# Hybrid attention trunk on one core: loads at the stages' turns, a copy on ScalarE, sums of squares on VectorE, stores in pairs, wider warming products

## The chip, the core and the metric

The kernel runs on one core of a Trainium2 chip. Times are device microseconds (us) of one execution. The engines are named as in the profile: PE is TensorE's matmul, PEld its weight load, DVE is VectorE, ACT is ScalarE, POOL is GpSimd, SP is SyncE, which issues most DMAs. L12 is line 12 of the kernel.

## What is computed

One layer over x (1024 x 2048, float32), with a second input p (1024 x 256):

```python
hn = rmsnorm(h, norm_mix_g); proj = hn @ w_in        # q, k, v, gate of 8 + 8 heads
sb_out = stick_breaking_attention(sb_q, sb_k, sb_v)   # sigmoids and a running product
df_out = differential_attention(rope(df_q), rope(df_k), df_v, lam)  # softmax1 - lam * softmax2
df_out = rmsnorm(df_out, subln_g) * (1 - lambda_init)
mixed = concatenate([sb_out * silu(sb_g), df_out * silu(df_g)])
h = h + mixed @ w_out
gate = sigmoid(rmsnorm(h, norm_ple_g) @ w_ple_gate)
out = rmsnorm(h + gate * (p @ w_ple_proj), norm_final_g)
```

## The kernel before

**Products.** Activations lie transposed, 128 features x 512 tokens to a tile; the 1024 tokens are two halves. Each float32 operand is split into two fp32r parts: ScalarE casts the high part, VectorE subtracts it from the original for the low part. Each product is then three matmuls: high x high, high x low, low x high (in the q/k projection L251 to L253). Most of the 11110 matmuls are these. The projections to v and gate, to the output, and to the last gate take Strassen's form with seven block products, A11, A12, S2, S1, S3, S4, A22 (class `Seven`): sums of blocks come from VectorE, and a result that is finished later is added up in DRAM or out of `part_d`.

**Stages, in time.** (1) v and gate for all 16 heads, up to about 640 us, both phases `ph` of 16 units; the four u's of a product are summed into PSUM tiles `pbc`, `pc`. (2) The heads of half 1, which attend to 512 keys, then, from about 1070 us ("the middle"), those of half 0, which attend to 1024, half 1's keys and values among them (kept in DRAM). For each head PE runs the q/k projection of that head as a stream of 32 groups of three matmuls (`unit`), and between the groups the attention of the head before it. `ORDER` alternates a differential head (`df`) and a stick-breaking head (`sb`); one such pair takes about 72 us in half 0. (3) From about 1650 us the output projection (8 units), (4) from about 2010 us the gate projection with products p1/p2 (A11, A12), p6 (S2), p5 (S1), p3 (S4), the S3 product, and A22, (5) final norm and stores.

**What sets the order.** PE's order is written out by hand (`manual_schedule`). Inside a head, `Side` holds steps with due times: after each group of three matmuls `side.tick()` runs what is due, and the table TICK (L41 to L54) gives the times in ticks. So a number in TICK decides behind which other instruction of its own engine a cast, a copy or a subtraction is issued; each engine takes its instructions in that order. In the Seven stages a slot (`op.slot`, `gv.slot`) is one block product; `soon` holds functions for a later slot, `xq` the operands to be loaded and split. SP issues its DMAs in order, each when its tile is free.

**The places that the change and the prediction touch:**
- Start: `warm` (L857) makes 24 products of the ones matrix, 128 columns each, while the first operands are loaded; the first real product is L647 to L649 (`Seven.product`), and L628 casts the first operands.
- Chores (L1043): from slot 36 of stage 1 on, w_out and parts of w_in are split ahead of time: slots of remainder 0 by three load a tile, of remainder 1 cast it and subtract (`chi`, `clo`, L1055), of remainder 2 store both to DRAM. L1110 adds PSUM's `pbc` to `s` in the last units of that stage.
- `wprep` (L160) loads a piece of w_in into `wraw`, casts `whi` (L172) and makes or loads `wlo` (L168, L174); `Stream` hands these out.
- Attention (a helper, L300 on): `scores` make z; for an sb head `weights` issues the sigmoids L358/L359, the scan L365 and the product L369; for a df head the masked minimum L382, the exponential L390 (`et`), the factors L395/L396 and the scaling L397, L402. `values` transposes v (L417), copies its high part (L419), subtracts its low part (L422). `turn` transposes weights (`tp`, L437), `parts` splits them (`lead`, `awh`: L455/L456; `awl`: L460/L461); `mix` multiplies them with v (`av`, L479 to L484) and sums the result (L495, L498; `avb`); `squared` (L511 to L514) makes `sqv`, `sqh`.
- A head's q and k (`taken`): for a df head they are copied from `acc` by ScalarE, rotated on VectorE (L1451 to L1454), cast (L1431, L1433, L1435) and their low parts subtracted (L1440). For an sb head q is copied by ScalarE (L1399), k is multiplied with `rstd` on VectorE (L1403: `qk<-acc,ssa`). v and gate of a head are loaded and multiplied with `rstd` (L1385).
- Output projection: `wf` tiles (`wfhi`, `wflo`, loads L1323) come from `wout_d`; the last head's result `mixed_d` is stored in L280; L647 to L649 read the weights.
- Gate stage: `norm` (L1770) multiplies two tiles of partial sums of squares with the ones matrix into one PSUM tile (L1775), and `load_sums` (L1790) loads the two tiles. `p6` (L1898) loads `part_d[u]` into `s` (L1902), forms S2's product, and adds (L1905); L1913 adds the product of p5. `gprod` is L1762 to L1764. `first_load` (L1518) loads both k halves of a weight block, `gate_operand` (L1234) the operands. 
- End: the last quarter of the output is transposed, scaled by the row's root (`leave`, L2169: L2174 on ScalarE, L2176 on VectorE), and stored by 8 DMAs (L2179, L2182); `finals` (L1986/L1987) adds and stores the columns ahead of it.

## Time and profile before

| | us |
|---|---|
| three timed runs | 2359.87, 2366.0, 2360.83 |
| their median | 2360.83 |
| the profiled execution, its own time | 2364.5 |
| its span | 2362.7 |
| busy: PE, DVE, ACT, POOL | 2324.6, 1796.3, 1269.2, 296.0 |
| granted TensorE clock, mean | 0.995 |
| DMA, mean | 236 GB/s |

A row of the list of waits reads: engine, tile and line that waited, what released it, then total us, how many times, the longest. A row of the table by stretch reads: start and end, length, then the busy time of PE, PEld, DVE, ACT, POOL with the count of instructions in brackets, then the granted clock of TensorE (1.00 is full), the DMA engines' busy share and GB/s. A row in order of time reads: start, busy time, engine, line, operation, output and inputs, shapes, and in square brackets the idle time before it and who ended that. A row of DMA issues ends with KB each and the us from issue to landing.

### The profile page before, as it was taken

The numbers are of one execution on the slowest core, as the hardware profiler recorded it, in microseconds if no ns is written. First come the engines' busy times: TensorE is split into PE (matmuls) and PEld (weight loads), VectorE is DVE, ScalarE is ACT, GpSimd is POOL, SyncE is SP. The second block draws the span as 40 slices with busy tenths as digits, with TensorE's granted clock in tenths as the row PEclk, the third lists the DMA queues.
The fourth block names the chain that finished last, engine by engine and source line by source line (L and its number), as shares of the span: only waits on it lengthen the run. The fifth ranks groups of instructions, "written<-read, shape, count | busy, mean of one in ns | idle before, by whom it ended". The sixth has DMA issues, their size and how long they took to land. (4 is left out here: it accounts for less than half of the span.)

```text
span 2362.7 us, 32655 instructions
## 1 busy us (share of the span) xinstructions
PE 2324.6 (98%) x11110; PEld 1937.1 (82%) x11110; DVE 1796.3 (76%) x3115; ACT 1269.2 (54%) x2305; POOL 296.0 (13%) x439
## 2 busy tenths in 40 slices
PE   9999999999999999999999999999899999999998
PEld 7878878888788888887888888888778887788787
DVE  7487786656578888877877877778687887687787
ACT  6323253333357776777767676677533434533455
POOL 2121111111100000000011100111021121111000
PEclk9999999999999999999999999999999999999999
DMA  8586798766787777787567666668798788998965
GB/s 263 205 292 230 256 302 219 196 144 131 208 276 245 248 249 256 256 302 241 197 194 212 180 188 209 196 196 255 220 248 213 245 242 267 307 353 271 327 201 183
DMA packets 255544, 556.66 MB, mean 236 GB/s; under 512 B 28544, under 2 KB 40064, under 8 KB 255376
## 3 DMA queue, kind: packets, MB, share of 16 engines
q1 hardware_dynamic: 186112, 396.18, 50.7%
q0 software_dynamic: 52848, 128.74, 22.3%
q10 hardware_dynamic: 16416, 29.65, 3.5%
q8 instruction: 87, 1.43, 0.2%
q14 instruction: 81, 0.66, 0.1%
HBM read 359.16 MB, written 203.69 MB: 238 GB/s over the span
## 5 line engine op out<-in xcount | busy, mean ns | idle before, releaser
L740 ACT CAST wpr<-T 128x512 fp32r<-128x512 f32 x208 | 127.2, 621 | 484.5 <-DVE T L699 402.2
L251 PE MATMUL acc<-xh,whi 128*128 128x512 f32 x768 | 314.5, 410 | 3.4 <-DVE qk L1403 3.2
L253 PE MATMUL acc<-xh,wlo 128*128 128x512 f32 x768 | 302.2, 393 | 0.9 <-DVE wlo L168 0.5
L252 PE MATMUL acc<-xl,whi 128*128 128x512 f32 x768 | 301.2, 392 | 0.0
L253 PEld LDWEIGHTS acc<-xh,wlo 128*128 128x128 f32 x768 | 144.6, 188 | 34.5 <-DMA wlo<-wlo_d 1.2
L251 PEld LDWEIGHTS acc<-xh,whi 128*128 128x128 f32 x768 | 145.2, 189 | 28.0 <-DVE qk L1403 3.6
L252 PEld LDWEIGHTS acc<-xl,whi 128*128 128x128 f32 x768 | 145.4, 189 | 23.5 <-issue 0.2
L172 ACT CAST whi<-wraw 128x1024 fp32r<-128x1024 f32 x128 | 134.6, 1052 | 23.8 <-DMA wraw<-w_in 9.3
L754 DVE TENSOR_TENSOR wpr<-T,wpr 128x512 fp32r<-128x512 f32 x208 | 142.5, 685 | 5.9 <-ACT wpr L740 2.7
L853 POOL DMA_DIRECT2D vg_d<-hc x128 | 89.1, 696 | 456.4 <-DVE hc L1072 267.3
L740 ACT CAST wpr<-wraw 128x512 fp32r<-128x512 f32 x128 | 78.8, 617 | 114.8 <-DMA wraw<-tw_d 35.6
L390 ACT ACTIVATE et<-z,mx 128x512 f32<-128x512 f32 (+7 forms) x128 | 94.7, 740 | 62.8 <-DVE mx L382 62.7
L456 ACT CAST awh<-tp 128x256 fp32r<-128x256 f32 (+1 forms) x160 | 81.0, 507 | 78.7 <-PE tp L437 78.7
L382 DVE CUSTOM_DVE_ANT_0 z<-z,wide 128x512 f32<-128x512 f32 (+7 forms) x128 | 97.5, 762 | 17.9 <-PE z L335 16.3
L461 DVE TENSOR_TENSOR awl<-tp,awh 128x256 fp32r<-128x256 f32 (+1 forms) x160 | 92.2, 576 | 23.6 <-ACT awh L456 21.2
L365 DVE TENSOR_TENSOR_SCAN pt<-pt 128x511 f32<-128x511 f32 (+3 forms) x64 | 86.7, 1355 | 28.2 <-ACT pt L358 27.6
L754 DVE TENSOR_TENSOR wpr<-wraw,wpr 128x512 fp32r<-128x512 f32 x128 | 86.9, 685 | 26.3 <-ACT wpr L740 26.2
L168 DVE TENSOR_TENSOR wlo<-wraw,whi 128x1024 fp32r<-128x1024 f32 x56 | 68.3, 1220 | 12.8 <-ACT whi L172 12.4
L358 ACT ACTIVATE pt<-z,rcol 128x511 f32<-128x511 f32 (+3 forms) x64 | 47.5, 742 | 52.7 <-DVE z L345 52.2
L484 PE MATMUL av<-awl,v 128*128 128x256 f32 x256 | 72.9, 285 | 1.5 <-DVE awl L461 1.5
L482 PE MATMUL av<-awh,v 128*128 128x256 f32 x256 | 72.4, 283 | 0.1
L483 PE MATMUL av<-awh,v 128*128 128x256 f32 x256 | 72.5, 283 | 0.0
(571 smaller groups left out, 6925.3 us busy)
## 6 DMA issues: line engine op xcount, KB each, us to landing
wraw<-w_in SPq DMA_DIRECT2D x128, 512.0 KB, 4.6
wlo<-wlo_d SPq DMA_DIRECT2D x72, 512.0 KB, 3.4
wraw<-w_vg SPq DMA_DIRECT2D x143, 256.0 KB, 3.6
vg_d<-hc POOLq DMA_DIRECT2D x128, 256.0 KB, 4.9
wlo_d<-wlo SPq DMA_DIRECT2D x56, 512.0 KB, 3.2
wraw<-w_gate SPq DMA_DIRECT2D x92, 256.0 KB, 5.5
h_d<-hc POOLq DMA_DIRECT2D x56, 256.0 KB, 4.9
wraw<-w_out SPq DMA_DIRECT2D x56, 256.0 KB, 4.5
```

Source lines behind the costliest of these rows:

```text
L172: side.later(1, lambda: A.copy(hi[:, o], raw[:, o]))
L251: T.matmul(acc[c], hi[:, k2, kh, c, :], xh, start=first, stop=False)
L252: T.matmul(acc[c], hi[:, k2, kh, c, :], xl, start=False, stop=False)
L253: T.matmul(acc[c], lo[:, k2, kh, c, :], xh, start=False, stop=last)
L365: V.tensor_tensor_scan(pt[:, w], pt[:, w], pt[:, w], initial=1.0, op0=ALU.mult, op1=ALU.bypass)
L382: V.tensor_tensor_reduce(z[:, vw], z[:, vw], add, -DF_SCALE, 3.0e38, ALU.add, ALU.min, mx)
L390: A.activation(et[:, vw], z[:, vw], AF.Exp, bias=mx[:, 0:1], scale=-1.0, accum_out=l[:, c:c + 1])
L456: A.copy(wh[:, o, :], tp[:, o, :])
L461: V.tensor_tensor(wl[:, o, :], tp[:, o, :], wh[:, o, :].bitcast(F32), op=ALU.subtract)
L740: A.copy(t[:, 0], src)
L754: V.tensor_tensor(t[:, 1], src, t[:, 0].bitcast(F32), op=ALU.subtract)
L853: G.dma_start(vg_d[hf, blk, u], o, **(dict(accum_op=ALU.add) if ph else {}))
```

## The change

It has these parts, told in the order of time.
- Warming: 9 products of 512 columns (the ones matrix repeated four times) in place of 24 of 128.
- Chores: a tile is loaded in a slot of remainder 0, cast and subtracted in that of remainder 2, stored in the next of remainder 0; no load in slots 78 to 86.
- The stream's first pieces of w_in are loaded at slots where weight blocks of stage 1 become free (`free`, `Stream.ahead`), rather than with a split `prep`.
- Ticks: the v copies (`vparts`) go from (1, 2) to (3, 4); the df exponential and scaling (`df_soft`) from (1.5, 2, 4.5, 6) to (1, 1.5, 4, 5.5); v and gate of an sb head (`sb_vg`) 2 to 2.5 ticks earlier; q of a df head (`q_turn`) about 2 ticks earlier; two entries of A11 and one of S1 move; the last entry of `begun` goes from 92.5 to 93.5. New entries with "mid_" and "end_" hold the same numbers as those without.
- Middle: in the last pair of the second half of the tokens, an sb head's k is copied by ScalarE and then multiplied on VectorE.
- Gate: the weight block of `first_load` is loaded one k half at a time; the operands of S3 are issued after the latest load in `op.lastw`, and p6's load of `part_d` sets `op.lastw`.
- Norms: one product with the ones matrix; the two sums of squares are added on VectorE two slots after their load is issued (L1822 of the changed kernel).
- End: the stores go out as two of 128 x 1024 and four of 128 x 512 (two column blocks each), and both last `finals` come ahead of them.

```diff
+    "sumlag": 2, "gvx": ((22, 27), (80, 85)), "chore": (36, 78, 87), "opx": (8, 12), ...
-    "parts": (1, 2), "vparts": (1, 2), ... "df_soft": (1.5, 2.0, 4.5, 6.0),
+    "parts": (1, 2), "vparts": (3, 4), ... "df_soft": (1, 1.5, 4, 5.5),
-    "sb_vg": (6, 17, 18, 26, 27.5), "q_turn": (1.5, 5, 7, 8.5, 12, 14, 15.5),
+    "sb_vg": (4, 15, 16, 24, 25.5), "q_turn": (-1.0, 5, 5, 6.5, 10, 12, 13.5),
...
+    def wraw_of(wsrc, pc):
+        raw = wp.tile([P, 2, 2, 2, P], F32, name="wraw", tag="wraw", bufs=2)
+        nc.sync.dma_start(raw, wsrc[pc])
+        return raw
...
+        def ahead(self):
+            self.raws.append(wraw_of(*self.todo[len(self.raws)][:2]))
...
-        for _ in range(24):
-            T.matmul(warm[:, :P], onesr, onesr, start=True, stop=True)
+        for _ in range(9):
+            T.matmul(warm.rearrange("p (a b) -> p a b", a=4), onesr, onesr.unsqueeze(1).to_broadcast([P, 4, P]), start=True, stop=True)
...
+        gv.free = {12: stream.ahead, 21: stream.ahead}
...
         def chore(slot):
-            if slot < CHORE or slot % 3 == 2 and not work:
-                return
-            if slot % 3 == 0 and chores:
+            if slot % 3 == 0 and done:
+                (hi, lo), hi_d, lo_d = done.pop()
...
+            if slot % 3 == 0 and chores and slot >= TICK["chore"][0] and not TICK["chore"][1] <= slot < TICK["chore"][2]:
...
-            elif slot % 3 == 1 and work:
+            elif slot % 3 == 2 and work:
...
-        piece0 = stream.prep(later=True)
         rest_of(prev, True)
-        piece0()
+        stream.prep()
         rest_of(prev, False)
...
-            eng.dma_start(lo.bitcast(F32), src)
+            if nm == "S3":
+                with tc.issue_after(op.lastw.ins):
+                    eng.dma_start(lo.bitcast(F32), src)
+            else:
+                eng.dma_start(lo.bitcast(F32), src)
...
-                            V.tensor_tensor(f, acc[c], rstd, op=ALU.mult)
+                            if seam == "mid_":
+                                A.copy(f, acc[c])
+                                V.tensor_tensor(f, f, rstd, op=ALU.mult)
+                            else:
+                                V.tensor_tensor(f, acc[c], rstd, op=ALU.mult)
...
-            for i, t in enumerate(tiles):
-                T.matmul(ps, ones, t, start=i == 0, stop=i == len(tiles) - 1)
+            T.matmul(ps, ones, out, start=True, stop=True)
...
+            op.soon.append((op.slot + TICK["sumlag"], lambda: V.tensor_tensor(r[0], r[0], r[1], op=ALU.add)))
...
-            nc.sync.dma_start(w, part_d[u])
+            op.lastw = nc.sync.dma_start(w, part_d[u])
...
-        leave(zA[:, 0, :], 0, 0, A)
-        leave(ps[0], 1, 0, V)
-        leave(zA[:, 1, :], 0, 1, A)
-        finals(7)
-        leave(zB[:, 0, :], 2, 0, A)
+        for j in range(2):
+            o = wp.tile([P, 2, HALF], F32, name="ow", tag="wraw", bufs=2)
+            leave(zA[:, j, :], o[:, 0, :], j, A)
+            leave(ps[j], o[:, 1, :], j, V)
+            nc.sync.dma_start(out_of(0, 4, j), o)
...
-        leave(ps[1], 1, 1, A)
-        leave(pt_[0], 3, 0, V)
-        leave(zB[:, 1, :], 2, 1, A)
-        leave(pt_[1], 3, 1, A)
+        for k, t in ((2, [zB[:, j, :] for j in range(2)]), (3, pt_)):
+            for j in range(2):
+                o = ftile()
+                leave(t[j], o, j, (A, V)[j])
+                nc.sync.dma_start(out_of(2 * k, 2, j), o.rearrange("t (c f) -> t c f", c=2))
```

## The prediction

> **What bounds the kernel now.** I read the profile's page first, then the list of TensorE's waits, then the table of busy time by stretch at the places that list names, and last the order in time around each of them.

> ```profile
> span 2362.7 us, 32655 instructions
> PE 2324.6 (98%) x11110; PEld 1937.1 (82%) x11110; DVE 1796.3 (76%) x3115; ACT 1269.2 (54%) x2305; POOL 296.0 (13%) x439
> ...
> PE av L479 <- DVE awl L461: 3.4, 8, 1.6
> PE pa L649 <- DMA wflo<-wout_d: 3.2, 1, 3.2
> PE acc L251 <- DVE qk L1403: 3.2, 1, 3.2
> PE pc L1762 <- DVE hc L1913: 2.7, 1, 2.7
> PE tp L437 <- DVE avb L498: 2.1, 8, 0.3
> ...
> PE av L484 <- DVE awl L461: 1.5, 2, 1.3
> PE pbc L647 <- DVE u L1110: 1.0, 1, 1.0
> ```

> TensorE (PE) is idle for 2362.7 - 2324.6 = 38.1 us of the span; no other engine comes near it. So an edit can win only by issuing less on PE, by shortening one of these waits (columns: total us, times, longest), or by keeping PE's clock up. That last part is in the table by stretch (PE busy in the third column, granted clock after the engines):

> ```profile
> 1069.10:1076.00 6.90, 5.77 (x17) 4.90 (x18) 6.38 (x16) 5.07 (x10) 0.68 (x1) 0.51 0.93 287
> ...
> 1659.70:1663.10 3.40, 3.40 (x15) 3.10 (x15) 1.18 (x3) 0.00 (x0) 0.00 (x0) 0.50 1.06 365
> ...
> 1693.80:1697.20 3.40, 3.40 (x11) 2.72 (x9) 2.18 (x4) 1.86 (x4) 0.85 (x1) 0.50 0.02 3
> ...
> 2222.90:2226.30 3.40, 3.15 (x8) 2.53 (x9) 2.72 (x5) 1.59 (x3) 0.70 (x2) 0.50 1.04 386
> ```

> Behind each of the long waits the clock is halved for 3.4 us, at 1069 for 6.9, twice that; 3.4 us at half clock do 1.7 us less work. So a long wait costs its idle time and 1.7 us more.

> **The change part by part.** The order in which the changed kernel's instructions stand was set beside the old one, engine by engine: PE's order is the same except for the warming products and three norm products that are gone.

> (a) *Start.* 24 warming products of 128 columns become 9 of 512.

> ```profile
> L858 PE MATMUL warm<-onesr x24: 415/415/475, 1.0 to 6.0; 128*128 128x128 f32 x24
> ...
> 6.17 0.73 PE L647 MATMUL pa<-cA11h,wfh 128*128 128x512 f32 x1
> ...
> 10.97 0.43 PE L649 MATMUL pa<-cA11h,wfl 128*128 128x512 f32 x1
> 11.48 0.39 PE L648 MATMUL pa<-cA11l,wfh 128*128 128x512 f32 x1
> 11.70 0.39 PE L649 MATMUL pa<-cA11h,wfl 128*128 128x512 f32 x1
> ...
> 6.15 0.72 ACT L628 ACTIVATE cA11h<-x,gvec 128x512 fp32r<-128x512 f32 x1 [1.34 <-DMA x<-xT]
> ```

> From 6.17 to 10.97 there are eleven steps of about 0.43 us, so nine warmers end near 1.0 + 9 x 0.43 = 4.8, 1.3 us sooner. But the second operand waits for its DMA and exists only at 6.15 + 0.72 = 6.87. If the twelve products still run at half clock behind it, 0.2 us is won; if half of them run at 0.22 us (the step from 11.48 to 11.70), 0.2 + 6 x 0.2 = 1.4. I take 0.5, nearer the first, since PE would stand idle until 6.87 for most of a 3.4 us stretch. [...]

> (b) *Chores at the turn of the first projection.* Loads are left out in slots 78 to 86, and each split comes one slot later.

> ```profile
> 334.15 0.68 DVE L1055 TENSOR_TENSOR clo<-craw,chi 128x512 fp32r<-128x512 f32 x1
> 334.75 0.68 DVE L1110 TENSOR_TENSOR u<-pbc,s 128x512 f32<-128x512 f32 x1
> ```

> PE waits 1.0 us for L1110, behind L1055, which is gone from there: 1.0 us won (0, if another write takes its place, to 1.2).

> (c) *Early w_in loads.* Around 600 to 645 us the order of SP, ScalarE and VectorE is the same, instruction for instruction. 0.

> (d) *Middle: k copied by ScalarE.*

> ```profile
> 1068.43 0.19 ACT L390 ACTIVATION_READ_ACCUMULATOR et<-z,mx 128x1 f32 x1
> 1069.49 0.68 DVE L1403 TENSOR_TENSOR qk<-acc,ssa 128x512 f32<-128x512 f32 x1
> ...
> L1399 ACT COPY qk<-acc 128x512 f32<-128x512 f32 x16 | 9.3, 582 | 0.5 <-PE acc L253 0.5
> ```

> PE is released by L1403's end at 1070.17. The copy stands right behind L390: 1068.52 + 0.58 = 1069.10, so PE goes on 1.1 us sooner. It then works through all of the next 3.4 us, and the second half-clock stretch should fall away: 1.7. Against it, L397 now stands between the copy and L455/L456 and waits for VectorE's L396 behind the rescaled k; awl comes about 1.2 us later, just when PE asks for it, up to 0.7 at half clock. I take 1.1 + 1.7 - 0.6 = 2.2 (0.7, if the second stretch stays, to 3.4).

> (e) *Ticks in the attention.* In half 0 each pair of heads has the same two small waits:

> ```profile
> 1176.00:1248.20 72.20, 71.68 (x389) 61.17 (x388) 56.66 (x99) 50.05 (x86) 7.98 (x11) 1.00 0.67 193
> ...
> 1174.30 1.75 DVE L365 TENSOR_TENSOR_SCAN pt<-pt 128x767 f32<-128x767 f32 x1 [1.38 <-ACT pt L358]
> ...
> 1169.62 0.59 ACT L456 CAST awh<-tp 128x512 fp32r<-128x512 f32 x1 [3.37 <-PE tp L437]
> ```

> That is 72.20 - 71.68 = 0.52 us a pair, seven times: 3.6. The scan L365 waits 1.38 us for ScalarE's L358, which stands behind q's four casts (L1431, L1433). With these ahead, L358, the scan and L461 come up to 1.4 us sooner, and L1440 no longer stands ahead of L498. Both waits are shorter than 1.4, so I take 3.6 (0 to 3.6). What is moved back pays from its slack. The tightest I find is v's low part (L422) in a differential head, now behind L461 and a normalisation like L1385:

> ```profile
> 1213.27 0.41 DVE L461 TENSOR_TENSOR awl<-tp,awh 128x256 fp32r<-128x256 f32 x1
> ...
> 1214.52 0.68 DVE L1385 TENSOR_TENSOR vf<-vf,ssa 128x512 f32<-128x512 f32 x1
> ...
> 1215.64 0.39 PE L479 MATMUL av<-lead,v 128*128 128x256 f32 x2
> ```

> 1213.68 + 0.68 + 0.69 = 1215.1 against 1215.64: 0.5 us are left.

> (f) *Into the output projection.* Near 1616, where PE waits 1.3 us for L461 (L484's row above), L461 moves ahead of one 0.7 us low part: 0.7 won (0 to 1.3). Near 1690 is the longest wait of L479, 1.6 us; a low part moves out from before the scan there: 0.6 (0 to 2.3, with the half-clock stretch after it). But on SP the store of mixed_d now stands ahead of the wflo load that PE waits 3.2 us for:

> ```profile
> wflo<-wout_d SPq DMA_DIRECT2D x1, 512.0 KB, 12.1
> mixed_d<-sg SPq DMA_DIRECT2D x1, 256.0 KB, 13.5
> ...
> 1647.29 0.50 SPq L1323 DMA_DIRECT2D wflo<-wout_d  x1
> 1647.88 0.45 SPq L280 DMA_DIRECT2D mixed_d<-sg  x1
> ```

> wflo landed at 1647.29 + 12.1 = 1659.4 and mixed_d at 1661.4: in that crowd a store takes 2.0 us. In front, it makes PE wait 2.0 longer. I take -2.0 (-2.7 with some half clock, 0 if the order of transfer does not follow the order of issue). Together -0.7.

> (g) *Norms.* One f32 product of the ones matrix is gone in each of three norms; VectorE adds the two sums instead (0.7 us, loaded well ahead).

> ```profile
> L1775 PE MATMUL ssps<-sums,onesr x12: 591/592/593, 2009.9 to 2268.7; 128*128 128x512 f32 x12
> ```

> Twelve records are six products of two passes; a norm has four of them, 0.43 us from start to start as in (a), and loses 0.86. The first and third are on the path: 1.7 (0.9 to 2.6). The second runs ahead of the wait of (h) and wins nothing by itself.

> (h) *Into S3.* The load of s from part_d now goes ahead of the S3 operands.

> ```profile
> 2205.58 0.37 SPq L1902 DMA_DIRECT2D s<-part_d  x1
> ...
> 2210.22 0.69 DVE L1905 TENSOR_TENSOR s<-pb,s 128x512 f32<-128x512 f32 x1 [6.19 <-DMA s<-part_d]
> ```

> VectorE waits 6.19 us for s, and PE later 2.7 us for L1913 behind it (first fence). With s ahead of them L1905 comes sooner, but the S3 operands, which were ahead, come later by its transfer and issue, and VectorE's splits of them stand ahead of L1913. I take 0.8, two issues of 0.37 us, between 0 and 2.5 (nearly the whole wait).

> (i) *Last stores.* Eight become six, and the eighth u's final goes out first.

> ```profile
> 2352.96 1.31 SPq L2179 DMA_DIRECT2D out_dram<-hc  x3
> ...
> 2356.57 1.94 SPq L2182 DMA_DIRECT2D out_dram<-ot  x3
> ...
> out_dram<-ot SPq DMA_DIRECT2D x4, 256.0 KB, 3.2
> ```

> The last issue was 2357.9. Now the first store needs two evictions, side by side on ScalarE and VectorE, so it goes out near 2353.2, and five issues of 0.65 us later, at 2356.5, the last; 3.2 later it lands. The store that ends it is 1.4 sooner by issue, less if the queue's bytes bind; I take 0.9 (0.3 to 1.3). [...]

> **Sum.** 0.5 + 1.0 + 0 + 2.2 + 3.6 - 0.7 + 1.7 + 0.8 + 0.9 = 10.0. The profiled execution took 2364.5 us (1.8 around the span); the median of the three is 2360.8, 3.7 lower. The sum is made in the profiled one, 2354.5, and carried over: 2350.8. Low ends add to -0.6, high ends to 19.6; they will hardly meet, and half of the way from the middle to either end gives 2346 to 2356.

> **The rivals.**
> *The small waits stay.* For (e): the casts that moved up are themselves behind VectorE's rotation of q, so L358 may come no sooner. 3.6 and the uncertain 2.0 of (f) and (d) go: 4.4 won, 2356.4. Against it stands that ScalarE sits idle for 3.4 us before 1169.62 (the row in (e)), room for those casts.
> *Fewer half-clock stretches.* Every seam's wait shrinks enough to keep the clock, or the stretch falls otherwise: the table shows three more than (d) counts on (1659, 1693, 2222): 3 x 1.7 = 5.1 more, 2345.7. [...]
> *The change moves nothing.* Turns stay as late as they were, as (c) shows for one; only removed work counts: 0.2 + 1.7 + 0.3 = 2.2, 2358.6.
> *Slower.* v's low part comes too late in each of the 16 turns of a differential head (8 in each half). It has 0.5 us; from 1.1 us later than I place it the loss of 0.63 a turn eats the 10.0; a wait as long as the one that PE has for L461 at 1616 costs 1.3 x 16 = 20.8: 2350.8 + 20.8 = 2371.6. VectorE is 76% busy on the whole, which speaks for it; that nothing but 0.7 us casts stand in between speaks against it.

> **How the numbers follow.** Forecast 0.49, small waits stay 0.20, fewer half-clock stretches 0.10, nothing moves 0.10, slower 0.11. A measurement tells 0.3% from no change, 7.1 us: faster means below 2353.7. Of the forecast's chance 0.39 lies below that, of the first rival's 0.04, all of the second's: 0.53. Within: 0.10 + 0.16 + 0.10 = 0.36. Slower 0.11. The range 2344 to 2360 leaves out the slower case and the outer edges of the others.

> **What would show it.** Right: seven pairs of 71.6 us without the two waits; no wait for L1110; the wait at 1066 for a ScalarE copy and one half-clock stretch behind it; L1775 six times; the wait for wflo about 5 us. Wrong: new waits for v or awl in every pair, or a wait for wflo at 3 us or less.

## The result, and the profile after

| | us (median, lowest to highest) | ratio to the kernel before, 95% interval |
|---|---|---|
| before, 5 runs | 2360.83 (2359.03 to 2366.0) | |
| changed, 5 runs | 2347.28 (2342.84 to 2351.72) | 0.9936 [0.9917, 0.9955] |

The medians lie 13.5 us apart, and the ratio with its interval says 0.64%: a little more than the 10.0 us forecast and inside the range. But the parts are not those of the sum: three came out far larger, one smaller, and one that stood at nothing costs 3.5 us.

The page of the changed kernel, and its list of TensorE's waits (in the changed kernel L402 is L418, L437 is L453, L460 is L476, L461 is L477, L479 is L495, L484 is L500, L498 is L514, L1110 is L1127, L1403 is L1425/L1426, L1440 is L1465, L1913 is L1941):

```profile
span 2341.1 us, 32641 instructions
PE 2310.1 (99%) x11089; PEld 1926.7 (82%) x11089; DVE 1795.1 (77%) x3120; ACT 1268.3 (54%) x2304; POOL 296.6 (13%) x439
...
PE av L495 <- DVE lead L476: 3.2, 7, 0.9
PE tp L453 <- DVE et L418: 1.8, 1, 1.8
...
PE pa L665 <- DMA wflo<-wout_d: 1.7, 1, 1.7
...
PE acc L269 <- DMA wlo<-wlo_d: 1.2, 1, 1.2
...
PE av L495 <- DVE awl L477: 1.1, 1, 1.1
...
PE acc L267 <- ACT qk L1425: 0.8, 1, 0.8
```

PE now idles 31.0 us in place of 38.1. The waits for awl in seven pairs, for avb, for L1110 and for L1913 are gone or short; those for lead (six in half 1, one in the middle) and the long one for et are new. The clock shows as much as the waits. These are the stretches of the changed kernel at the four places where the prediction's table had 0.50 (the middle, wflo, the scan before A12, S3):

```profile
1066.90:1073.80 6.90, 5.17 (x25) 3.77 (x24) 5.59 (x15) 5.09 (x13) 0.68 (x1) 1.00 0.81 276
...
1650.40:1653.80 3.40, 3.17 (x19) 2.87 (x20) 1.47 (x4) 0.91 (x2) 0.00 (x0) 1.00 1.10 268
...
1682.60:1686.00 3.40, 3.40 (x19) 2.89 (x19) 2.45 (x4) 2.04 (x4) 0.85 (x1) 1.00 0.33 60
...
2204.00:2207.40 3.40, 3.40 (x16) 2.80 (x15) 1.50 (x3) 2.71 (x4) 0.89 (x1) 1.00 1.05 389
```

All five half-clock stretches that the old trace has ahead of PE's last product (the one in the middle counts twice) are gone: 5 x 1.7 = 8.5 us at most, for in the middle it was worth less, as shown further down.

**Where the time went.** Without the warming and the norms, both kernels run the same 11040 products on PE in the same order. So the start of each product in one trace can be set against its start in the first trace of the kernel before. What that offset gains within a stage is what the stage won (minus) or lost. All in us, the bounds in the time of the first trace of before:

| stage | forecast | before, 2nd trace | changed | changed, 2nd trace |
|---|---|---|---|---|
| start, to 100 | -0.5 | -0.5 | -1.4 | -1.1 |
| turn of the first projection, 300 to 420 | -1.0 | -0.1 | -1.9 | -1.9 |
| half 1, 688 to 1041 | 0 | 0.0 | +3.5 | +3.5 |
| middle, 1041 to 1107 | -2.2 | 0.0 | -1.0 | +0.2 |
| half 0, 1107 to 1611 | -3.6 | 0.0 | -6.5 | -6.5 |
| into the output projection, 1611 to 1745 | +0.7 | +0.8 | -5.9 | -4.3 |
| into the gate, 1975 to 2000 | 0 | -0.1 | -1.2 | -1.4 |
| first and third norm | -1.7 | 0.0 | -1.7 | -1.7 |
| ple products, 2018 to 2060 | 0 | -1.6 | -1.6 | -1.6 |
| S3, 2200 to 2262 | -0.8 | -0.9 | -3.4 | -2.8 |
| behind PE's last product | -0.9 | 0.0 | -0.7 | -0.7 |

With 0.1 elsewhere the column of the changed kernel's first trace adds up, before rounding, to 21.7, the difference of the two spans. The medians differ by 13.5. The old profile was 3.7 us above its median, and the new one is the fastest of its five runs; the row of the ple products, alike in all other traces, is chance of the first one. So the stages are read from several traces below, not from one pair.

### The profile page after: what moved, and what is told of

Same layout as the page of the kernel before. It is cut to its first block, busy times and chain, and to the rows that moved or that the text cites. A ratio compares the mean times of both kernels' runs of the same rounds, so it can differ in the third digit from the quotient of the medians.

```text
span 2341.1 us, 32641 instructions
## 1 busy us (share of the span) xinstructions
PE 2310.1 (99%) x11089; PEld 1926.7 (82%) x11089; DVE 1795.1 (77%) x3120; ACT 1268.3 (54%) x2304; POOL 296.6 (13%) x439
## 5 line engine op out<-in xcount | busy, mean ns | idle before, releaser
L477 DVE TENSOR_TENSOR awl<-tp,awh 128x256 fp32r<-128x256 f32 (+1 forms) x160 | 92.3, 577 | 40.9 <-ACT awh L472 40.4
L500 PE MATMUL av<-awl,v 128*128 128x256 f32 x256 | 72.9, 285 | 1.0 <-DVE awl L477 1.0
L413 ACT ACTIVATE et<-et,l 128x512 f32<-128x512 f32 (+3 forms) x64 | 49.4, 772 | 42.8 <-DVE l L412 42.8
L498 PE MATMUL av<-awh,v 128*128 128x256 f32 x256 | 72.1, 282 | 0.2
## 6 DMA issues: line engine op xcount, KB each, us to landing
wraw<-w_in SPq DMA_DIRECT2D x128, 512.0 KB, 4.7
wlo<-wlo_d SPq DMA_DIRECT2D x72, 512.0 KB, 3.5
wraw<-w_vg SPq DMA_DIRECT2D x143, 256.0 KB, 3.7
vg_d<-hc POOLq DMA_DIRECT2D x128, 256.0 KB, 4.9
wlo_d<-wlo SPq DMA_DIRECT2D x56, 512.0 KB, 3.7
wraw<-w_gate SPq DMA_DIRECT2D x92, 256.0 KB, 5.3
h_d<-hc POOLq DMA_DIRECT2D x56, 256.0 KB, 5.1
wraw<-w_out SPq DMA_DIRECT2D x56, 256.0 KB, 4.7
```

The lines of the kernel that those rows point to most:

```text
L477: V.tensor_tensor(wl[:, o, :], tp[:, o, :], wh[:, o, :].bitcast(F32), op=ALU.subtract)
```

## The experiments

Unless said otherwise each kernel is the changed one with the edit shown. Ratios are to the kernel before, run on the same chip.

**A second look at both kernels.** No edit.

> The changed kernel once more, beside which the next kernels are read. If the two profiles shown so far are typical, its time is 2343 to 2352 us and PE's offsets against the kernel before are those of the first trace (start -1.4, turn of the first projection -1.9, half 1 +3.4, half 0 -6.4, into the output projection -4 to -6, gate -8). Rival: part of the 21 us between the two profiled spans is chance (the medians are only 13.5 apart), then some half-clock stretches stand elsewhere in this trace and its span is 3 to 8 us longer.

> The kernel before once more, for a second trace. Its profiled execution was 3.7 us above its median. Theory: the difference is in half-clock stretches behind the long waits of the way into the output projection (1611 to 1745 us) and of the gate, which fall differently from run to run; here the span is near 2358 us and one or two of the stretches at 1659, 1693 and 2222 are shorter. Rival: the stages take the same in every run, and the span is again 2362 to 2363.

Measured: changed 2347.53 us, 0.9948 [0.9935, 0.9960]; the second trace of before spans 2359.9 us. The last two columns of the table are theirs. Before's half-clock stretches stand in the same four places again (granted 0.52 from 1067.8 to 1074.7, 0.60 in the 3.4 us from 1657.9 and from 1692.0, 0.76 from 2220.0, none of these laid on the grid described below), against the theory, and its span is 2.8 us shorter, against the rival: by the ple products (1.6), S3 (0.9), the start (0.5) and 0.6 in smaller pieces, less 0.8 on the way into the output projection. So the stretches belong to that kernel. In the changed kernel one of them, behind the wait for et, is there in one trace and not in the other, with the same wait of 1.84 us. First the changed kernel's first trace, then its second (the wait, then the table by stretch in steps of 3.41 us):

```profile
1080.44 0.33 PE L453 MATMUL tp<-ident,et 128*128 128x128 f32 x1 [1.84 <-DVE et L418]
...
1075.98:1079.39 3.41, 2.61 (x15) 1.93 (x14) 3.34 (x10) 1.87 (x5) 0.55 (x1) 1.00 1.03 368
1079.39:1082.80 3.41, 2.36 (x11) 1.98 (x12) 2.02 (x7) 3.41 (x9) 0.88 (x1) 1.00 0.99 243
...
2335.50:2338.90 3.40, 0.00 (x0) 0.00 (x0) 0.00 (x0) 0.00 (x0) 0.00 (x0) 0.50 1.00 348
```

```profile
1080.69 0.33 PE L453 MATMUL tp<-ident,et 128*128 128x128 f32 x1 [1.84 <-DVE et L418]
...
1077.48:1080.89 3.41, 1.57 (x10) 1.09 (x10) 3.09 (x9) 2.04 (x4) 1.43 (x2) 1.00 1.03 364
1080.89:1084.30 3.41, 3.41 (x10) 2.64 (x10) 2.27 (x7) 3.09 (x10) 0.00 (x0) 0.50 0.91 196
```

Half-clock stretches start on a grid: in the first trace of before the granted clock is 0.50 from 1659.67 to 1663.08, 3.41 us, and the prediction's rows at 1659.7, 1693.8 and 2222.9 lie 34.1 and 529.1 apart, 10.0 and 155.0 times 3.413 (1659.67 to 2222.87 is 563.2, 165 steps of 3.413). The first trace's only low stretch stands behind PE's last product, at 2335.5; counted back from there in steps of 3.413 (368 of them), a step ends at 1079.39 and cuts the wait in two, and PE is busy for 2.61 and 2.36 of each 3.41. In the second trace the whole wait lies in one step, PE is busy for 1.57 of 3.41, and the next step runs at half clock: here 1.84 us of idle in a step of 3.41 were followed by a granted clock of 0.50.

**q's ticks in half 1.**

```diff
-side.add(zip(TICK[seam + "qk"[c] + "_turn"], steps))
+side.add(zip(TICK[seam + "qk"[c] + "_turn"] if c or half == 0 else (1.5, 5, 7, 8.5, 12, 14, 15.5), steps))
```

> q_turn of the kernel before in half 1 only, the new one in half 0. Theory: in half 1 one of q's low parts (0.69 us on VectorE) now stands ahead of the scan, so lead comes 0.68 us later and PE waits for it 0.55 us in each of six pairs. With the old ticks there the six waits go: 3.3 us faster than the changed kernel, while half 0 keeps its 0.92 us a pair. Rival: the waits come from the v copies or the exponentials, whose ticks stay; then nothing changes.

> The kernel with the old q_turn in half 1 once more, beside which the next two are read: near 2344 us, half 1 without the six waits.

Measured: 2344.06 us, 0.9934 [0.9922, 0.9947], and 2344.2 us, 0.9930 [0.9917, 0.9943]. Half 1 comes out at -0.4 in both traces in place of +3.5; all else stays. First VectorE before the change (709 to 715 us), then VectorE and the waiting product in the changed kernel:

```profile
711.46 0.68 DVE L1454 TENSOR_TENSOR qk<-qk,sw 128x512 f32<-128x512 f32 x1
712.06 1.21 DVE L168 TENSOR_TENSOR wlo<-wraw,whi 128x1024 fp32r<-128x1024 f32 x1
713.30 0.69 DVE L1440 TENSOR_TENSOR q<-qk,q 64x512 fp32r<-64x512 f32 x1
714.02 0.69 DVE L365 TENSOR_TENSOR_SCAN pt<-pt 128x255 f32<-128x255 f32 x1
714.66 0.29 DVE L460 TENSOR_TENSOR lead<-tp,lead 128x128 fp32r<-128x128 f32 x1
714.87 0.41 DVE L461 TENSOR_TENSOR awl<-tp,awh 128x256 fp32r<-128x256 f32 x1
715.31 0.69 DVE L1440 TENSOR_TENSOR q<-qk,q 64x512 fp32r<-64x512 f32 x1
```

```profile
707.44 0.69 DVE L1465 TENSOR_TENSOR q<-qk,q 64x512 fp32r<-64x512 f32 x1
708.05 0.28 DVE L361 TENSOR_TENSOR z<-z,masks 128x128 f32<-128x128 f32 x1
...
710.83 0.69 DVE L1465 TENSOR_TENSOR q<-qk,q 64x512 fp32r<-64x512 f32 x1
711.55 0.69 DVE L381 TENSOR_TENSOR_SCAN pt<-pt 128x255 f32<-128x255 f32 x1
712.16 0.27 DVE L476 TENSOR_TENSOR lead<-tp,lead 128x128 fp32r<-128x128 f32 x1
...
712.48 0.50 PE L495 MATMUL av<-lead,v 128*128 128x256 f32 x2 [0.38 <-DVE lead L476]
```

VectorE has no bracket in these rows, so it does not idle here: every instruction in front of lead moves it. Before, one of q's two low parts (L1440) stood behind awl, at 715.31; now both (L1465) stand ahead of the scan, and lead comes 0.6 to 0.7 later against PE. PE waits 0.38 us in each of six pairs, and a pair is 0.43 to 0.66 us longer than before, 3.5 us in all.

**The other ticks, and q's ticks everywhere.**

```diff
-"vparts": (3, 4), "df_soft": (1, 1.5, 4, 5.5), "sb_vg": (4, 15, 16, 24, 25.5)
+"vparts": (1, 2), "df_soft": (1.5, 2.0, 4.5, 6.0), "sb_vg": (6, 17, 18, 26, 27.5)
```

> vparts, df_soft and sb_vg as in the kernel before; q_turn stays new. Theory: q_turn alone makes both the loss in half 1 (six waits of 0.55 us) and the gain in half 0 (0.92 us a pair, seven pairs), so both stay and the time is within 1.5 us of the changed kernel. Rival: these three entries make one or the other; then the six waits go (3.3 us faster) or half 0 loses part of its 6.4 us.

Measured: 2347.08 us, 0.9945 [0.9932, 0.9959]. Half 1 loses 3.9 and half 0 wins 6.5, against 3.5 and 6.5 in the changed kernel. (The middle is 3.1 slower there: PE waits 3.3 us for a load of wlo.)

```diff
-"q_turn", "mid_q_turn", "end_q_turn": (-1.0, 5, 5, 6.5, 10, 12, 13.5)
+"q_turn", "mid_q_turn", "end_q_turn": (1.5, 5, 7, 8.5, 12, 14, 15.5)
```

> q_turn of the kernel before everywhere, all other parts as changed. Theory: q_turn alone makes the gain of half 0; the seven pairs are as long as in the kernel before (6.5 us more than in the changed kernel) and half 1 has no waits for lead (3.5 us less): 3 us slower than the changed kernel. Rival: other ticks share in half 0's gain; then part of the 0.92 us a pair stays.

Measured: 2349.51 us, 0.9951 [0.9938, 0.9964]. Half 0 is back at 0.0, half 1 at -0.4. The waits for lead of the other ticks' kernel, then the waits for awl and avb of this one:

```profile
PE av L495 <- DVE lead L476: 2.7, 6, 0.5
```

```profile
PE av L495 <- DVE awl L477: 2.8, 8, 1.0
...
PE tp L453 <- DVE avb L514: 2.1, 8, 0.3
```

So q_turn alone makes both: it gains 0.92 us a pair in half 0, where VectorE stood idle for 1.38 us, and loses in half 1, where it had no room. The rows of such a pair before the change show why 0.92 and not 0.52:

```profile
1610.40 0.47 PE L479 MATMUL av<-lead,v 128*128 128x256 f32 x2 [0.26 <-DVE awl L461]
1611.49 0.66 PE L437 MATMUL tp<-ident,bt 128*128 128x128 f32 x4 [0.27 <-DVE avb L498]
```

The idle times in brackets are 0.26 and 0.27, but with the waits gone PE gains 0.42 at each of these two products and 0.08 and 0.06 at the ones right behind them: each wait costs about 0.2 more than its listed idle. (A little of the 0.98 goes again within the pair.)

**The copy in the middle.**

```diff
-if seam == "mid_":
+if seam == "none_":
```

> The middle's k is again multiplied out of PSUM on VectorE; all else as in the changed kernel. By the prediction's step the copy is worth 2.2 us (0.7 to 3.4), so this is 2.2 us slower. Rival, read from the trace: the copy takes away 2.4 us of PE's wait, but ScalarE's scaling of et then stands ahead of lead and awh, and PE waits 0.9 us for lead and 1.8 us later for et; without the copy these two waits go and the loss is 1 us or less.

Measured: 2346.0 us, 0.9938 [0.9926, 0.9951], so not slower than the changed kernel; its middle is at +0.5. With the copy the middle came out between -1.0 and +0.9 in ten traces (and at +3.1 in the other ticks' kernel). Neither expectation holds as a whole. The wait for lead is gone, but the one for et is there without the copy too, and in this trace PE had waited 2.6 us for a load of wlo before. First the changed kernel's waits in the middle (the one for et, 1.84 us at 1080.44, is quoted further up), then this kernel's:

```profile
1068.72 0.50 PE L267 MATMUL acc<-xh,whi 128*128 128x512 f32 x1 [0.81 <-ACT qk L1425]
1071.65 0.51 PE L495 MATMUL av<-lead,v 128*128 128x256 f32 x2 [0.92 <-DVE lead L476]
```

```profile
PE acc L269 <- DMA wlo<-wlo_d: 2.6, 1, 2.6
...
PE tp L453 <- DVE et L418: 1.8, 1, 1.8
```

So the middle has three waits in a row, for wlo, for k's accumulator and for et, and what PE saves at one it spends at the next: in the changed kernel 1.2, 0.8 and 1.8 us, in the second trace with the old q_turn in half 1 0.4, 2.4 and 1.2, in the kernel with the old q_turn everywhere none, 2.9 and 0.3. These are the last kernel's rows:

```profile
1066.11 0.79 PE L267 MATMUL acc<-xh,whi 128*128 128x512 f32 x1 [2.87 <-ACT qk L1425]
1077.82 0.33 PE L453 MATMUL tp<-ident,et 128*128 128x128 f32 x1 [0.31 <-DVE et L418]
```

From the product that k's copy releases to the product that waits for et it is 11.71 us here and 11.72 in the changed kernel (1068.72 to 1080.44), although the clock is halved for most of 6.8 us in between here (granted 0.50 from 1065.5 to 1072.3) and not at all there. It is 11.7 in nine of the ten traces with the copy (11.5 in the tenth, the last kernel below) and 11.3 in both traces of before. So et comes at a fixed distance behind the release, and a half-clock stretch between the two costs PE nothing at et: without it PE waits there longer. The release itself came 1.1 to 1.8 us sooner within the stage in these ten traces than in the first one of before, near the 1.1 that was forecast; how much of that is the copy's, the one trace without it, late by its wait for wlo, can't tell. From there to et 0.4 is lost (0.2 in the last kernel), and behind et another 0.5, or 1.6 where the clock falls there (0.0 in the last kernel): that makes the range of -1.0 to +0.9.

**The store and S3.**

```diff
-nc.sync.dma_start(mixed_d[half, hd], t)
+(held.append if (half, hd) == (0, 6) else (lambda f: f()))(lambda: nc.sync.dma_start(mixed_d[half, hd], t))
...
+i and held and held.pop()()
...
-                with tc.issue_after(op.lastw.ins):
-                    eng.dma_start(lo.bitcast(F32), src)
```

> Two edits far apart: the store of mixed_d again behind the wflo load that PE waits for (1655 us), and the operands of S3 loaded without waiting for p6's load of s (2200 us). First: by the prediction's step PE goes on 2.0 us sooner at wflo. Rival: what sets that wait is when the store to part_d lands, for which SP stands still before the wf loads, and where the crowd of transfers stands; then the swap changes PE by less than 0.7 us. Second: the load of s is again late, PE waits 2.7 us for L1913's addition and a half-clock stretch follows: 4 us slower there. Rival: 0.8 us, as predicted.

Measured: 2346.69 us, 0.9940 [0.9925, 0.9955]. PE waited 0.6 us for wflo, against 1.7 and 2.2 in the two traces of the changed kernel, which looked like the prediction's step at half its size; the last two kernels below tell whether it is. For S3 the wait for L1913's addition (L1937 here) is back, but the stage is at -1.8 against -3.4 and -2.8 in the changed kernel, a loss of 1.0 to 1.6 us and not of 4, for the clock did not fall (granted 0.999 on the mean of this trace, against 0.995 in both of before). These are this kernel's waits, then the one for that addition in the first kernel with the old q_turn in half 1, where the loads of S3 stand as changed:

```profile
PE pc L1786 <- DVE hc L1937: 1.9, 1, 1.9
...
PE pa L665 <- DMA wflo<-wout_d: 0.6, 1, 0.6
```

```profile
PE pc L1790 <- DVE hc L1941: 1.5, 1, 1.5
```

The second one stands against putting the whole loss down to the order of the loads. Of the eleven traces with the changed order ten have no such wait, but S3 comes out anywhere between -1.2 and -3.4 in them (-1.5 in the one with the wait), so one trace with the old order at -1.8 does not show what the order is worth. Part of what is won goes again at the two waits for qt (L2057 and L2080), 0.3 and 1.2 us in the changed kernel's first trace, 1.1 and 0.9 in its second, where before there was one of 0.2 or none.

**The ends.** The 24 narrow warmers, the old chores, two products a norm and eight stores, all back in one kernel.

```diff
-        for _ in range(9):
+        for _ in range(24):
...
-            elif slot % 3 == 2 and work:
+            elif slot % 3 == 1 and work:
...
-            T.matmul(ps, ones, out, start=True, stop=True)
+            for i, t in enumerate(tiles):
+                T.matmul(ps, ones, t, start=i == 0, stop=i == len(tiles) - 1)
...
-        finals(6, 7)
+        finals(6)
```

> Four edits undone whose places lie far apart, so that each can be read in the trace by itself: 24 narrow warming products, the old order of the chores, two products in each norm, eight last stores. By the traces so far: start 1.2 us slower on the mean of the runs (0 to 1.4, it varies with the same code), the turn at 335 us 1.9 slower, each norm 0.86 slower on PE, of which the second runs ahead of a wait, the end behind PE's last product 0.8 slower; 5 us in all. By the prediction: 0.5 + 1.0 + 1.7 + 0.9 = 4.1 us.

Measured: 2348.02 us, 0.9947 [0.9931, 0.9964]. Start +0.1, turn -1.1, both norms on the path 0.0, the end as before the change (10.0 us from the start of PE's last product, against 9.4). So a norm's product is worth 0.86 us each, twice, the stores 0.6, warming 0.8 on the mean of eleven traces with wide and three with narrow products (0.0 to 1.4), and the chores 1.3 on the same mean (-1.7 against -0.4; 0.8 by this kernel beside the changed one). The chores are the least certain of these: here the split stands ahead of L1110's addition again, yet PE waits only 0.3 us for it, and in three of the eleven traces with the new order PE waits for it too, 0.2 to 0.7 us, and the turn wins 0.9 to 1.4 in place of 1.7 to 1.9.

**The operands' ticks.** On top of the old q_turn in half 1:

```diff
-"A11": (.., (9.6, 16), ..), "S1": (.., (58.5, 70), ..), "begun": (86.5, 91.5, 93.5, 94.5, 93.5)
+"A11": (.., (8.6, 15), ..), "S1": (.., (58.5, 73), ..), "begun": (86.5, 91.5, 93.5, 94.5, 92.5)
```

> On top of the old q_turn in half 1: the changed entries of A11, S1 and begun back to those of the kernel before. The way into the output projection (1611 to 1745 us) came out 5 to 8 us faster than in the first trace of before, where the prediction had a loss of 0.7. Theory: these entries move two casts' low parts out from before awl and the scan, and so save the waits at 1616 and 1692 with their half-clock stretch: 2 to 3.5 us of the gain go again. Rival: the gain comes from the stream being earlier by q_turn, and from the DMA queue; then less than 1 us goes.

Measured: 2347.69 us, 0.9946 [0.9924, 0.9967], 3.6 above the kernel without this edit. But the four runs lie far apart, from 2343.3 to 2352.7 us, and the traced one is the longest, so this size is uncertain. The way into the output projection is at +1.5, against -5.3 and -3.5 in the two traces of that kernel. Its rows:

```profile
1608.41 0.39 PE L500 MATMUL av<-awl,v 128*128 128x256 f32 x1 [1.32 <-DVE awl L477]
...
1684.33 0.48 PE L495 MATMUL av<-lead,v 128*128 128x256 f32 x2 [1.65 <-DVE awl L477]
...
PE pa L665 <- DMA wflo<-wout_d: 3.8, 1, 3.8
...
1652.00:1655.40 3.40, 3.40 (x16) 3.07 (x16) 1.18 (x3) 0.14 (x1) 0.00 (x0) 0.61 1.07 348
1685.80:1689.20 3.40, 3.40 (x12) 2.77 (x11) 2.17 (x4) 1.84 (x4) 0.54 (x1) 0.56 0.04 7
```

The waits of 1.3 and 1.65 us for awl and both half-clock stretches are those of the kernel before. With the new entries they are 0.39 and 1.06 us (the second stands in the changed kernel's list above), and the clock stays up (1.00 in the changed kernel's stretches at the top). (The two rows of stretches here are not laid on the grid, so 0.61 and 0.56 are part full and part half clock.) The other traces bear the waits out: in the eleven with the new entries the two for awl are at most 0.39 and 1.06 us, in the three with the old ones at least 1.28 and 1.64; the wait for wflo is 0.6 to 2.7 us in the former and 3.0 to 3.8 in the latter.

**Two versions beyond the change.** The old q_turn in half 1 with the late store, and the same with the scaling of et half a tick later in the middle's differential head.

> The old q_turn in half 1, and the store of mixed_d again behind the wflo load. In the one trace with that swap PE waited 0.6 us for wflo, in five with the store ahead 1.0 to 3.8. Theory (the prediction's step, smaller): the wait is near 0.6 again, 1 us shorter and with less at half clock, 1 to 2 us faster than the kernel above. Rival: the 0.6 was one draw of a wait that depends on when the store to part_d lands; then the wait is 1 us or more here too.

> As the one above, and in the middle's differential head the scaling of et half a tick later, so that on ScalarE it stands behind lead, awh, k's cast and whi, as in the kernel before; k stays copied by ScalarE. Theory: of the two waits that came in the copy's place the one for lead (0.9 us) goes, the one for et (1.8 us) stays or grows up to 2 us: between 0.9 faster and 0.2 slower in the middle. Rival: both waits come from the copy itself, and neither changes.

```diff
-side.later(TICK["df_soft"][2], two)
+side.later(4.5 if (half, hd) == (1, ORDER[-2]) else TICK["df_soft"][2], two)
-side.later(TICK["df_soft"][3], three)
+side.later(6 if (half, hd) == (1, ORDER[-2]) else TICK["df_soft"][3], three)
```

Measured, the first with the diffs of q's ticks in half 1 and of the store above, the second with this one too: 2344.06 us, 0.9923 [0.9911, 0.9935], and 2342.35 us, 0.9921 [0.9909, 0.9933]. The kernel with only the old q_turn had 2344.2 in the same sitting, so neither is shown to be faster than it. All three medians lie 3 to 5 us below the changed kernel's; the intervals of the ratios overlap, but the traces show 3.9 of it in half 1. The wait for wflo in the first and in the second, and the second's wait for et:

```profile
PE pa L665 <- DMA wflo<-wout_d: 1.6, 1, 1.6
```

```profile
PE tp L453 <- DVE et L418: 2.8, 1, 2.8
...
PE pa L665 <- DMA wflo<-wout_d: 1.4, 1, 1.4
```

With the store behind the load the wait was 0.6, 1.6 and 1.4 us; with the store ahead, in the changed kernel's runs and in those with the operands' new ticks, 1.0 to 2.7. The order of the two is worth less than the wait differs from run to run. In the second's middle the wait for lead is gone and the one for et has grown from 1.8 to 2.8: et still comes 11.5 us behind the release, so PE gives back there what it saved at lead.

## Why the prediction was right, and where it was not

The sum was 10.0 and the medians give 13.5: the sign and the range held, but by errors that partly cancel.

- *Start* (0.5): 0.8 on the mean of the traces, between the 0.2 and the 1.4 that the step named. With the wide products PE comes to short steps sooner: in the changed kernel's first trace those from 6.47 on are 0.23 us where PE doesn't wait, against 0.43 until 10.97 before. That this is the clock is read from the steps alone: 0.43 is also the step at a granted 0.50 (1694.34 to 1696.48 in before), while the table by stretch has 1.00 from the start in both. PE then waits for the operands, as the step said (0.5 us for ScalarE's cast, 0.6 for VectorE's subtraction).
- *Turn* (1.0): 1.3 on the mean. L1055 left and the wait for L1110 with it, in eight of eleven traces; how much of it the chores make is not shown beyond that.
- *Early loads* (0): 0.1 between 420 and 688 us. Right.
- *Middle* (2.2): about 0.1 in the mean of ten traces with the copy. The first term (1.1) held: PE was released 1.1 to 1.8 us sooner. The step that failed is the second term, "It then works through all of the next 3.4 us, and the second half-clock stretch should fall away: 1.7". In the changed kernel both stretches behind the release did fall away, but et (L418, before L402) came 11.7 us behind it whether they were there, as with the old q_turn everywhere, or not, and 11.3 before; so PE reached et's product no sooner for it and waited up to 1.8 or 2.8 us there. The delay had been looked for in awl alone. What paces et itself stays open.
- *Ticks in the attention* (3.6): 6.5 in half 0 minus 3.5 in half 1, 3.0 net. In half 0 the mechanism was right and the size was off: the waits were priced at their listed idle (0.52 a pair), and they cost 0.92. In half 1 the step "what is moved back pays from its slack" was used for v's low part only, which never made PE wait more than 0.2 us. What lost its slack was lead, which is not in the list of moved instructions at all: something was moved ahead of it on an engine without idle time. The rival on the slower side had the right shape (a low part that comes too late, at 0.6 us a turn), but at another tile and in six turns of sixteen.
- *Into the output projection* (-0.7): 4.3 to 6.7 won (the changed kernel's two traces against the two of before). Two steps failed. "In front, it makes PE wait 2.0 longer": the wait for wflo went from 3.2 and 3.0 to 1.7 and 2.2 us, so the prediction's own sign of being wrong, a wait of 3 us or less, was there, and moving the store back changed nothing that can be told from the wait's own scatter. And the awl wait at 1692 was taken at 0.6, its half-clock stretch standing in the range alone: the wait went from 1.65 to 1.06 us, and the stretch behind it (1.7) vanished with that. What shortened the wait for wflo is shown only as far as that all traces with the operands' old ticks have 3.0 or more and none with the new ones; through which DMA stays open.
- *Norms* (1.7): 0.86 twice, exactly. *Stores* (0.9): 0.7.
- *S3* (0.8): 1.9 to 3.4 in the changed kernel's traces. The term was too small because it left the clock to a rival: the wait for L1913 with its half-clock stretch (1.7) is present in both traces of before and in none of the changed kernel. What of it is the order of the loads is not shown; the wait came back without the new order, but once with it too.
- *Into the gate* (0): 1.2 to 1.4 won, and 0.9 lost with a half-clock stretch there in the kernel with q's old ticks everywhere (granted 0.50 from 1987.1 to 1990.5) and in the one with the operands' old ticks. Why is open.

Of the rivals, "fewer half-clock stretches" (2345.7) is the one that happened, together with the forecast: it named the stretches at 1659, 1693 and 2222, and all three are gone. The measured 2347.3 lies between the two. That the sum came so near is luck in part: the 3.5 lost in half 1 hid about as much of what the stretches won.

## What to carry to other kernels

A tick that fills idle time in one stage delays what follows in a stage where the same engine has none: look at the engine's gaps in every stage that shares the number, and give the stages numbers of their own (here worth 3.5 us). Price a wait of the matmul engine at its idle time, plus about 0.2 us that the list doesn't show (here 0.42 + 0.08 against 0.26), plus the half-clock stretch (1.7 us here) where about half of a 3.4 us step is idle (here 1.88 of 3.41 us ahead of the scan's). A wait that ends earlier is only worth the distance to the next operand that has no slack (here et, 11.7 us behind the release).

## What the runs showed of the hardware

```profile
1656.29:1659.70 3.41, 0.26 (x1) 0.26 (x2) 0.03 (x1) 0.00 (x0) 0.00 (x0) 1.00 1.10 263
1690.39:1693.80 3.41, 1.53 (x12) 1.09 (x10) 3.41 (x7) 0.81 (x2) 0.84 (x1) 1.00 1.10 339
2219.49:2222.90 3.41, 0.97 (x3) 0.14 (x1) 3.38 (x6) 1.30 (x3) 0.00 (x0) 1.00 1.06 384
```

PE is busy for 1.53 of 3.41 in the second: 0.6 us less idle, as in the changed kernel, saves that and the 1.7 of the stretch, 2.3 us. The grid's phase differs from run to run: a step ends at 1079.39 in the changed kernel's first trace and at 1080.89 in its second, 1.50 apart. Whether that is part of why the same kernel's times spread over 9 us (2342.84 to 2351.72) is not shown.
